# Split weights of the post stage: written to DRAM in the first pass, loaded as parts in the later ones

## The chip, the cores and the metric

The kernel runs on one NeuronCore of a Trainium2 chip. The metric is the device time of one execution in microseconds. The engines are TensorE (PE: matrix products), VectorE (DVE), ScalarE (ACT), GpSimd (POOL) and SyncE (SP), which issues nearly all DMAs. SBUF is the memory on the chip, PSUM holds the accumulators of PE, and DRAM is the memory outside.

## The reference

One layer of a bidirectional encoder, float32, 2048 tokens of 1024 numbers:

```
y = rmsnorm(h, norm_mix_g) @ w_in                  # q, k, v (8 heads of 64), conv input and gate
att  = dilated_sliding_attention(q, k, v)          # three windows: (128,1), (512,4), (2048,16)
conv = conformer_conv(a, g, ...)                   # gated, 31 taps, layernorm, silu
h = h + concat([att, conv]) @ w_out
xq = rmsnorm(h, norm_x_g) @ w_xq;  mn = rmsnorm(mem, norm_mem_g)     # 256 memory rows, 4 heads of 256
h = h + softmax(xq (mn @ w_xk)^T / 16) (mn @ w_xv) @ w_xo
u = rmsnorm(h, norm_mlp_g) @ w_up                  # 1024 -> 4096
h = h + square(relu(u)) @ w_down                   # 4096 -> 1024
return rmsnorm(h, norm_final_g)
```

## The kernel before

Every product is made in float32 quality from float16 parts. A number is held as a high part and a low part (what the high part leaves over), both float16, and `mm3` sums three products: high by high, high by low, low by high. Activations and weights are split alike. For a weight tile of 128 x 1024 float32 the split is two instructions in `wsplit2`: ACT writes the scaled tile as float16 (L362), and DVE takes it from the scaled float32 tile and writes the rest as float16 (L363). The two parts together are as large as the float32 tile, 512 KB.

The kernel works in stages. A first stage normalises x, multiplies by `w_in`, prepares the memory side (from w_xq, w_xk, w_xv, w_xo it builds two matrices once, `ascr` and `bscr`, in DRAM) and scans the weights for scales. Attention for the first 512 tokens follows. Then comes the post stage, in four passes `p` of 512 tokens each, function `post(p)`. A pass multiplies by w_out (8 tiles), by the memory matrices a and b (8 tiles each), by w_up (32 tiles) and by w_down (32 tiles), with norms between them. The weights don't fit into SBUF, so each pass loads every tile anew. `wpost` does that:

```
raw = wp.tile(list(shape), F32, tag="raw", name=f"raw_{name}", bufs=3)
dma(raw, src)
n = turn_w[0]
turn_w[0] += 1
return two(wsplit2(wq if n % 4 > 1 else wp, raw, name, scale, shape=shape))
```

There are three buffers for raw tiles and four for split ones: two in the pool `wp`, two in the pool `wq`, taken in turn. One tile serves 24 matmuls of 128x512. `ahead(m)` prepares the first two tiles of w_out while the first attention still runs.

Beside pass `p` run attention (`att`) and convolution (`conv`) of the next 512 tokens, woven in by rate. Attention fills PE where the main work waits, and uses DVE (scores with mask, `att_probs`, L1042), ACT (exponentials L1043), PE (turning L1049, products L1057 to L1059, scores L1260). Convolution is 30 DVE instructions of `cacc` (L392) for each 128 x 512. Before the MLP the norm's chain runs: column sums (nps, L1449), a reciprocal root on DVE and POOL (`rstd_col`: st_v, nr, st_t, L346 to L353), its broadcast on PE (nrb, L358), ACT's copy ssumx (L1577), and then `rl` on DVE (L1596), which reads the accumulator of a w_up tile with that scale.

The last pass, `last_mlp`, has no attention beside it. It multiplies by w_down with seven products instead of eight (`seven`), in seven pieces of 128 x 2 x 512 for each of its first seven groups; `quarter` loads the four quarters of w_down that the pieces are made of, `sums` adds and subtracts them, and `piece` splits the results. `hidden` makes the w_up products.

The program is written in this order, but a scheduler that models time places each instruction in its engine's queue; each engine then runs its queue strictly in order, SP too. A DMA that has to wait holds up all later DMAs of its queue.

Of the kernel before, what the change touches and what calls it, by code (L numbers as in the profile page):

```python
# [12 lines left out]
F16 = mybir.dt.float16  # L13
# [8 lines left out]
P = 128  # L22
# [12 lines left out]
KC = D // P  # L35
# [13 lines left out]
def hybrid_layer(ctx, tc, A, out):  # L49
# [7 lines left out]
    def dma(o, i, q=None):  # L57
        (q or nc.sync).dma_start(o, i)

    dr = pool("dram", DRAM)  # L60
# [55 lines left out]
    cath = [dr.tile([P, S], F16, name=f"cath{k}") for k in range(KC)]  # L116
    catl = [dr.tile([P, S], F16, name=f"catl{k}") for k in range(KC)]
    gscr = [dr.tile([P, 2, 8, P], F16, name=f"gscr{i}") for i in range(8)]
    vscr = dr.tile([P, 2, 8, 256], F16, name="vscr")
    ascr = dr.tile([XH // 2, P, KC, 2 * NMEM], F32, name="ascr")  # L120
    bscr = dr.tile([KC, P, KC, P], F32, name="bscr")
# [92 lines left out]
    S_UP, S_DN, S_OUT, S_A, S_B = (bcol(i) for i in range(5))  # L214
# [3 lines left out]
    K_OUT, K_A, K_B, K_UP, K_DN = (bcol(24 + i) for i in range(5))  # L218
# [139 lines left out]
            PE.transpose(dst_ps[:, j * P:(j + 1) * P], col[:, j:j + 1].to_broadcast([P, P]), ident)  # L358

    def wsplit2(wp, raw, name, scale, shape=(P, 8, P)):  # L360
        t = wp.tile([P, 2, *shape[1:]], F16, tag="ws", name=f"ws_{name}", bufs=2)
        ACT.activation(t[:, 0], raw, AF.Copy, scale=scale)  # L362
        DVE.scalar_tensor_tensor(t[:, 1], raw, scale, t[:, 0], op0=ALU.mult, op1=ALU.subtract)  # L363
        return t

    def two(t):
        return t[:, 0], t[:, 1]

    def wcols(w, c0, n=P, rows=None):
        v = w.rearrange("(k p) m -> p k m", p=P)  # L370
        return v[:, :, c0:c0 + n] if rows is None else v[:, rows[0]:rows[1], c0:c0 + n]
# [7 lines left out]
    w_in, w_out = A["w_in"][0], A["w_out"][0]  # L379
    w_xq, w_xk, w_xv, w_xo = (A[n][0] for n in ("w_xq", "w_xk", "w_xv", "w_xo"))  # L380
    w_up, w_down = A["w_up"][0], A["w_down"][0]
# [73 lines left out]
    wp = pool("weights")  # L455
# [895 lines left out]

    turn_w = [0]

    def wpost(src, name, scale, shape=(P, 8, P)):

        raw = wp.tile(list(shape), F32, tag="raw", name=f"raw_{name}", bufs=3)
        dma(raw, src)
        n = turn_w[0]
        turn_w[0] += 1
        return two(wsplit2(wq if n % 4 > 1 else wp, raw, name, scale, shape=shape))  # L1360

    wout = {}

    def ahead(m):
        yield
        raw = wp.tile([P, 8, P], F32, tag="raw", name=f"raw_o0{m}", bufs=3)
        dma(raw, wcols(w_out, m * P))
        yield
        yield
        wout[m] = two(wsplit2(wp, raw, f"o0{m}", S_OUT))  # L1370
        turn_w[0] += 1
        yield

# [96 lines left out]
    def resid_linear(load, rhs, korder, resid, hs, ssum, scale, gains, y, name, steps=False, wide=False):  # L1470


        for ms in ((0, 1, 2, 3) if wide else (0, 1, 2), () if wide else (3,), (4,), (5,), (6,), (7,)):
            wt = [load(m) for m in ms]
            pts = {}
            cuts = (0, 4, 6, 7, 8) if wide else (0, 4, 6, 8)
            for ks in [korder[a:b] for a, b in zip(cuts, cuts[1:])] if len(ms) > 1 else (korder,):
                for m, (wh, wl) in zip(ms, wt):
                    if m not in pts:
                        pts[m] = ps("m3" if wide and m == 3 else "mm", f"{name}{m}")  # L1480
                    for k in ks:
                        mm3(pts[m], wh[:, k, :], wl[:, k, :], rhs["h", k], rhs["l", k], k == korder[0], k == korder[-1])
                    if steps and ks[-1] != korder[-1]:
                        yield
                    if ks[-1] == korder[-1]:
                        h = hs[m]
                        g = gains[:, m:m + 1]
                        last["dve"] = DVE.scalar_tensor_tensor(h, pts[m], scale, resid(m), op0=ALU.mult, op1=ALU.add)
                        ACT.activation(y["h", m], h, AF.Copy, scale=g)  # L1489
                        DVE.scalar_tensor_tensor(y["l", m], h, g, y["h", m], op0=ALU.mult, op1=ALU.subtract)  # L1490
                        add_sq(h, ssum, m == 0)
                        yield

    def post(p):
# [6 lines left out]
        def from_x(m):  # L1501
# [3 lines left out]

        y = ytiles("y")
        ssum = ssum_tile(f"o{p}")
        yield from resid_linear(lambda m: wout[m] if p == 0 and m in wout else wpost(wcols(w_out, m * P), f"o{p}{m}", S_OUT),
                                cats[p], [4, 5, 6, 7, 0, 1, 2, 3], from_x, hs, ssum, K_OUT, gxm[:, 0:8], y, f"o{p}_",
                                p == 0, p == 0)  # L1510
        rs = rstd_from(ssum)
# [31 lines left out]
        for hp in range(XH // 2):  # L1543
            pth, ptl = (xquad(q, hp, f"pt{q}{p}{hp}") for q in "hl")
            for e in range(4):
                pr_["h", 4 * hp + e], pr_["l", 4 * hp + e] = pth[:, e], ptl[:, e]
            sps = []
            for kk in range(4):
                ah, al = wpost(ascr[hp, :, 2 * kk:2 * kk + 2, :], f"a{p}{hp}{kk}", S_A, (P, 2, 512))
                for t in range(4):  # L1550
                    if kk == 0:
                        sps.append(ps("xs", "xs"))
                    js = slice(P * t, P * t + P)
                    for k2 in range(2):
                        k = 2 * kk + k2
                        mm3(sps[t], y["h", k][:, js], y["l", k][:, js], ah[:, k2, :], al[:, k2, :], k == 0, k == KC - 1)
                    if len(late) > 2 or (late and kk == 0):
                        turn_probs(*late.pop(0))
                    if kk == 3:
                        late.append((pth, ptl, t, soft(sps[t], t)))  # L1560
                yield
# [1 line left out]

        y = ytiles("m")
        ssum = ssum_tile(f"x{p}")
        xl = resid_linear(lambda m: wpost(bscr[m], f"b{p}{m}", S_B), pr_, list(range(KC)), lambda m: hs[m], hs, ssum, K_B,
                          gxm[:, 8:16], y, f"x{p}_", True)
        for _ in range(3):
            next(xl)
# [14 lines left out]
        for fg in range(FG):  # L1584
            hh = {}
            for q in "hl":
                t = xquad(q, fg % 2, f"hh{q}{p}_{fg}")
                for j in range(4):
                    hh[q, j] = t[:, j]
            for c in range(4):  # L1590
                wh, wl = wpost(wcols(w_up, fg * 512 + c * P), f"u{p}{fg}_{c}", S_UP)
                pt = ps("mm", "up")
                for k in range(KC):
                    mm3(pt, wh[:, k, :], wl[:, k, :], y["h", k], y["l", k], k == 0, k == KC - 1)
                r = tmp("rl")
                last["dve"] = DVE.scalar_tensor_tensor(r, pt, 0.0, rsb, op0=ALU.max, op1=ALU.mult)  # L1596
                ACT.activation(r, r, AF.Square)
                ACT.copy(hh["h", c], r)
                DVE.tensor_tensor(hh["l", c], r, hh["h", c], op=ALU.subtract)
                yield  # L1600
            if fg == FG - 1:
                fsum = ssum_tile(f"f{p}")
                load_cat(p + 1, 0)

            def down(mp2, wh, wl):
                for e in range(2):
                    m = 2 * mp2 + e
                    es = slice(P * e, P * e + P)
                    pt = ps("mm", "dn")
                    for k in range(4):  # L1610
                        mm3(pt, wh[:, k, es], wl[:, k, es], hh["h", k], hh["l", k], k == 0, k == 3)
                    last["dve"] = DVE.scalar_tensor_tensor(hs[m], pt, K_DN, hs[m], op0=ALU.mult, op1=ALU.add)  # L1612
                    if fg == FG - 1:
                        add_sq(hs[m], fsum, m == 0)

            for mp2 in range(4):
                down(mp2, *wpost(wcols(w_down, mp2 * 256, 256, (4 * fg, 4 * fg + 4)), f"d{p}{fg}_{mp2}", S_DN, (P, 4, 256)))
                yield


# [20 lines left out]
    def last_mlp(hs, y, rsb):  # L1641
# [24 lines left out]

        def hidden(fg, c):

            wh, wl = wpost(wcols(w_up, fg * 512 + c * P), f"u{p}{fg}_{c}", S_UP)
            pt = ps("up", "up")  # L1670
            for k in range(KC):
                mm3(pt, wh[:, k, :], wl[:, k, :], y["h", k], y["l", k], k == 0, k == KC - 1)
                if fg == 0 and c < 2 and k % 2:
                    to_rows(4 * c + k // 2)
            r = tmp("rl") if c else cv.tile([P, 512], F32, tag="vr", name="rl", bufs=2)
            last["dve"] = DVE.scalar_tensor_tensor(r, pt, 0.0, rsb, op0=ALU.max, op1=ALU.mult)
            ACT.activation(r, r, AF.Square)
            return r
# [42 lines left out]
            return t  # L1721

        def piece(w, name):
            n = turn_w[0]
            turn_w[0] += 1
            return two(wsplit2(wq if n % 4 > 1 else wp, w, name, S_DN, shape=(P, 2, 512)))

        def sums(b):

# [139 lines left out]
```

## Time and profile before

| | |
|---|---|
| time, median of 3 runs | 2739.62 us (2738.18 to 2741.42) |
| the profiled execution | 2743.33 us, of which the span of its instructions is 2741.6 us |
| busy | PE 97%, DVE 75%, ACT 48%, POOL 13% |
| DMA | 413.81 MB, 151 GB/s over the span |
| first w_out product of the post stage | 715.8 us after the start |
| granted clock of PE, mean | 0.988 |

A row of the profile names the line of the kernel, the engine, the operation, what it writes and reads (`out<-in`), shapes and count, then the busy time in us and the mean of one in ns, and behind the last bar the idle time of the engine just before, with what ended it. Matmuls overlap: one of 128x512 is shown as 380 ns long, but one starts every 215 ns, so a busy PE may still be slow when its clock is. `PEclk` is the share of the full clock that PE was granted. In the list of waits, a row says which engine and instruction waited for which, the sum in us, how often, and the longest.

### The profile page before, as it was taken

Reading aid. Unit: us, or ns where it says so; the run is one execution under the profiler, and the core shown is the slowest. Engines: PE = TensorE matmul, PEld = TensorE weight load, DVE = VectorE, ACT = ScalarE, POOL = GpSimd, SP = SyncE. Lnnn points to the kernel's source line nnn. Section 1 sums busy time; section 2 is a strip of 40 time slices with the busy share of each in tenths; the row PEclk is TensorE's granted clock in tenths of the full one; section 3 lists DMA queues with packets and bytes.
Section 4 is the critical chain, followed back from the end, with each engine's and each line's share of the span. In section 5 each row is a group of like instructions: output and inputs, shape, how many; then the busy total and the mean of one; then the engine's idle time right before and its main releaser. Section 6 shows DMA issues by size and latency. Waiting matters only on the chain.

```text
span 2741.6 us, 41228 instructions
## 1 busy us (share of the span) xinstructions
PE 2661.1 (97%) x15514; PEld 1454.8 (53%) x15514; DVE 2047.5 (75%) x3707; ACT 1315.3 (48%) x2185; POOL 345.5 (13%) x405
## 2 busy tenths in 40 slices
PE   8879999999899999999999999999999999999998
PEld 7734446777555445545554554455455544444443
DVE  5675665577689887667988966589887656679997
ACT  5625655376555434434543444355434434445543
POOL 1033201131200110310010113000110210000000
PEclk9979999999999999999999999999999999999999
DMA  9985888756544444445344445444444445223341
GB/s 269 279 209 175 249 254 279 202 146 197 141 132 120 128 129 127 138 135 169 101 129 136 123 127 139 139 145 124 122 123 144 129 138 176 92 86 99 101 123 62
DMA packets 534088, 413.81 MB, mean 151 GB/s; under 512 B 124957, under 2 KB 470993, under 8 KB 533120
## 3 DMA queue, kind: packets, MB, share of 16 engines
q1 hardware_dynamic: 525920, 396.15, 50.3%
q10 hardware_dynamic: 5744, 9.02, 1.0%
q0 software_dynamic: 2224, 6.01, 0.6%
q8 instruction: 122, 2.00, 0.3%
q14 instruction: 78, 0.64, 0.1%
HBM read 342.52 MB, written 68.57 MB: 150 GB/s over the span
## 4 chain that ended last, share of the span: by engine, by line
PE 65%; DVE 8%; DMA 3%; issue 3%; POOL 2%; ACT 1%; SPq 0%; DVEq 0%; POOLq 0%; ACTq 0%
PE dn L375 7%; PE dn L377 7%; PE dn L376 7%; PE up L375 7%; PE up L376 7%; PE up L377 7%; PE pt L1049 2%; PE xs L375 2%; PE xs L376 2%; PE xs L377 2%; DVE cacc L392 2%; PE s L1260 1%; PE o L375 1%; PE o L377 1%; PE o L376 1%
## 5 line engine op out<-in xcount | busy, mean ns | idle before, releaser
L375 PE MATMUL up<-mh,ws_u 128*128 128x512 f16 x1024 | 389.4, 381 | 0.7 <-ACT mh L1489 0.6
L376 PE MATMUL up<-ml,ws_u 128*128 128x512 f16 x1024 | 389.6, 380 | 0.0
L377 PE MATMUL up<-mh,ws_u 128*128 128x512 f16 x1024 | 388.4, 380 | 0.0
L392 DVE SCALAR_TENSOR_TENSOR cacc<-cu,cw,cacc 128x512 f32<-128x512 f32 x480 | 367.0, 765 | 4.9
L377 PE MATMUL dn<-hhh,ws_d 128*128 128x512 f16 x768 | 290.6, 379 | 0.0
L376 PE MATMUL dn<-hhl,ws_d 128*128 128x512 f16 x768 | 290.5, 379 | 0.0
L375 PE MATMUL dn<-hhh,ws_d 128*128 128x512 f16 x768 | 283.0, 379 | 0.9 <-DVE h L1612 0.9
L362 ACT ACTIVATE ws_u<-raw_u,bd 128x1024 f16<-128x1024 f32 x128 | 146.8, 1147 | 236.5 <-PE dn L377 186.9
L362 ACT ACTIVATE ws_d<-raw_d,bd 128x1024 f16<-128x1024 f32 x100 | 114.8, 1148 | 279.6 <-PE up L377 251.5
L1612 DVE SCALAR_TENSOR_TENSOR h<-dn,bd,h 128x512 f32<-128x512 f32 x192 | 140.6, 746 | 62.9 <-PE dn L377 60.1
L363 DVE SCALAR_TENSOR_TENSOR ws_u<-raw_u,bd,ws_u 128x1024 f16<-128x1024 f32 x128 | 163.9, 1280 | 19.3 <-ACT ws_u L362 17.1
L1042 DVE CUSTOM_DVE_ANT_0 sm<-s,mask,qks 128x256 f32<-128x256 f32 (+1 forms) x384 | 150.9, 434 | 30.5 <-PE s L1260 20.1
L377 PEld LDWEIGHTS <-ws_u 128*128 128x128 f16 x1024 | 100.4, 98 | 120.8 <-issue 1.8
L1596 DVE SCALAR_TENSOR_TENSOR rl<-up,ssumx 128x512 f32<-128x512 f32 x96 | 65.7, 690 | 131.1 <-PE up L377 131.1
L375 PEld LDWEIGHTS <-ws_u 128*128 128x128 f16 x1024 | 100.8, 98 | 114.9 <-issue 1.7
L376 PEld LDWEIGHTS <-ws_u 128*128 128x128 f16 x1024 | 101.0, 99 | 113.4 <-issue 1.4
L363 DVE SCALAR_TENSOR_TENSOR ws_d<-raw_d,bd,ws_d 128x1024 f16<-128x1024 f32 x100 | 133.8, 1338 | 31.2 <-ACT ws_d L362 30.6
L1043 ACT ACTIVATE sm<-sm,o 128x256 f32<-128x256 f32 (+1 forms) x288 | 116.3, 453 | 72.8 <-DVE o L1042 72.1
L1053 DVE TENSOR_TENSOR pl<-pt,ph 128x512 f16<-128x512 f32 x160 | 109.3, 685 | 37.4 <-ACT ph L1052 37.2
L377 PEld LDWEIGHTS <-ws_d 128*128 128x128 f16 x768 | 75.1, 98 | 89.1
L1052 ACT CAST ph<-pt 128x512 f16<-128x512 f32 x160 | 91.1, 571 | 60.0 <-PE pt L1049 59.9
L376 PEld LDWEIGHTS <-ws_d 128*128 128x128 f16 x768 | 75.1, 98 | 80.5 <-issue 2.5
(518 smaller groups left out, 6394.9 us busy)
## 6 DMA issues: line engine op xcount, KB each, us to landing
raw_u<-in_w_up_dram SPq DMA_DIRECT2D x128, 512.0 KB
raw_d<-in_w_down_dram SPq DMA_DIRECT2D x100, 512.0 KB
scan<-in_w_up_dram SPq DMA_DIRECT2D x32, 512.0 KB
scan<-in_w_down_dram SPq DMA_DIRECT2D x32, 512.0 KB
raw_o<-in_w_out_dram SPq DMA_DIRECT2D x32, 512.0 KB
raw_a<-ascr SPq DMA_DIRECT2D x32, 512.0 KB
raw_b<-bscr SPq DMA_DIRECT2D x32, 512.0 KB
b<-in_w_down_dram SPq DMA_DIRECT2D x28, 512.0 KB
```

The source lines that it names most:

```text
L362: ACT.activation(t[:, 0], raw, AF.Copy, scale=scale)
L363: DVE.scalar_tensor_tensor(t[:, 1], raw, scale, t[:, 0], op0=ALU.mult, op1=ALU.subtract)
L375: PE.matmul(o, lh, rh, start=first, stop=False, skip_group_check=more)
L376: PE.matmul(o, lh, rl, start=False, stop=False, skip_group_check=more)
L377: last["pe"] = PE.matmul(o, ll, rh, start=False, stop=end, skip_group_check=more)
L392: DVE.scalar_tensor_tensor(acc, u[:, t:t + 512], cw[:, c, t:t + 1], acc, op0=ALU.mult, op1=ALU.add)
L1042: last["dve"] = DVE.tensor_tensor_reduce(dst, so, mask[:, 256 * m:256 * m + nk], SCORE, 3e38, ALU.add, ALU.min, mn)
L1043: last["act"] = ACT.activation(dst, dst, AF.Exp, bias=mn, scale=-1.0)
L1052: ACT.copy(ph, pt)
L1053: DVE.tensor_tensor(pl, pt, ph, op=ALU.subtract)
L1596: last["dve"] = DVE.scalar_tensor_tensor(r, pt, 0.0, rsb, op0=ALU.max, op1=ALU.mult)
L1612: last["dve"] = DVE.scalar_tensor_tensor(hs[m], pt, K_DN, hs[m], op0=ALU.mult, op1=ALU.add)
```

## The change

The first pass still loads and splits every tile, and then writes the two parts to DRAM: 88 new arrays `wst` of 128 x 2048 float16, one for each tile of w_out, a, b, w_up and w_down. Passes 2 to 4 load the parts of a tile from `wst` straight into a split buffer, with no raw tile and no ACT or DVE work. In these passes the tiles take turns over seven buffers, the four split ones and the three that were raw. Tiles that are still split, in the first pass and the w_down pieces of the last, take turns over four. The counter is one for both. The last pass's w_down comes from the float32 weights as before, since its pieces are sums of quarters.

```
+    wst = [dr.tile([P, 2 * 1024], F16, name=f"wst{i}") for i in range(88)]
...
+    def wtile(name, n, shape):
+        i = turn_w[0] % n
+        turn_w[0] += 1
+        pl, tag, bufs = (wp, "ws", 2) if i < 2 else (wq, "ws", 2) if i < 4 else (wp, "raw", 3)
+        return pl.tile([P, 2, *shape[1:]], F16, tag=tag, name=f"ws_{name}", bufs=bufs)
...
-    def wpost(src, name, scale, shape=(P, 8, P)):
+    def wpost(src, name, scale, shape=(P, 8, P), key=None, p=0):
+        if p and key is not None:
+            t = wtile(name, 7, shape)
+            dma(flat(t), wst[key])
+            return two(t)
         raw = wp.tile(list(shape), F32, tag="raw", name=f"raw_{name}", bufs=3)
         dma(raw, src)
-        n = turn_w[0]
-        turn_w[0] += 1
-        return two(wsplit2(wq if n % 4 > 1 else wp, raw, name, scale, shape=shape))
+        t = split_to(wtile(name, 4, shape), raw, scale)
+        if key is not None:
+            dma(wst[key], flat(t))
+        return two(t)
...
-        wout[m] = two(wsplit2(wp, raw, f"o0{m}", S_OUT))
+        t = wsplit2(wp, raw, f"o0{m}", S_OUT)
+        dma(wst[m], flat(t))
+        wout[m] = two(t)
...
-                wh, wl = wpost(wcols(w_up, fg * 512 + c * P), f"u{p}{fg}_{c}", S_UP)
+                wh, wl = wpost(wcols(w_up, fg * 512 + c * P), f"u{p}{fg}_{c}", S_UP, (P, 8, P), 24 + 4 * fg + c, p)
...
         def piece(w, name):
-            n = turn_w[0]
-            turn_w[0] += 1
-            return two(wsplit2(wq if n % 4 > 1 else wp, w, name, S_DN, shape=(P, 2, 512)))
+            return two(split_to(wtile(name, 4, (P, 2, 512)), w, S_DN))
```

`split_to` is the body of `wsplit2` with the tile handed in, and `flat` names a tile's two parts as one row of 2048 in each partition. The other calls of `wpost` get a key and `p` in the same way as the one shown: w_out the keys 0 to 7, a 8 to 15, b 16 to 23, w_up 24 to 55, w_down 56 to 87.

More of the change, by code (lines that the diff above doesn't have):

```diff
@@ L360, in wsplit2, with split_to @@
     def wsplit2(wp, raw, name, scale, shape=(P, 8, P)):
-        t = wp.tile([P, 2, *shape[1:]], F16, tag="ws", name=f"ws_{name}", bufs=2)
+        return split_to(wp.tile([P, 2, *shape[1:]], F16, tag="ws", name=f"ws_{name}", bufs=2), raw, scale)
+    def split_to(t, raw, scale):
         ACT.activation(t[:, 0], raw, AF.Copy, scale=scale)
@@ L1352, in hybrid_layer, with flat @@
     turn_w = [0]
-    def wpost(src, name, scale, shape=(P, 8, P)):
+    def wtile(name, n, shape):
[3 more added lines that the diff above has]
+        return pl.tile([P, 2, *shape[1:]], F16, tag=tag, name=f"ws_{name}", bufs=bufs)
+    def flat(t):
+        return t.rearrange("p h a b -> p (h a b)")
+    def wpost(src, name, scale, shape=(P, 8, P), key=None, p=0):
[3 more added lines that the diff above has]
+            return two(t)
         raw = wp.tile(list(shape), F32, tag="raw", name=f"raw_{name}", bufs=3)
         dma(raw, src)
-        n = turn_w[0]
-        turn_w[0] += 1
-        return two(wsplit2(wq if n % 4 > 1 else wp, raw, name, scale, shape=shape))
+        t = split_to(wtile(name, 4, shape), raw, scale)
+        if key is not None:
+            dma(wst[key], flat(t))
+        return two(t)
     wout = {}
@@ L1507, in post @@
         ssum = ssum_tile(f"o{p}")
-        yield from resid_linear(lambda m: wout[m] if p == 0 and m in wout else wpost(wcols(w_out, m * P), f"o{p}{m}", S_OUT),
+        yield from resid_linear(lambda m: wout[m] if p == 0 and m in wout else wpost(wcols(w_out, m * P), f"o{p}{m}", S_OUT, (P, 8, P), m, p),
                                 cats[p], [4, 5, 6, 7, 0, 1, 2, 3], from_x, hs, ssum, K_OUT, gxm[:, 0:8], y, f"o{p}_",
@@ L1548, in post @@
             for kk in range(4):
-                ah, al = wpost(ascr[hp, :, 2 * kk:2 * kk + 2, :], f"a{p}{hp}{kk}", S_A, (P, 2, 512))
+                ah, al = wpost(ascr[hp, :, 2 * kk:2 * kk + 2, :], f"a{p}{hp}{kk}", S_A, (P, 2, 512), 8 + 4 * hp + kk, p)
                 for t in range(4):
@@ L1565, in post @@
         ssum = ssum_tile(f"x{p}")
-        xl = resid_linear(lambda m: wpost(bscr[m], f"b{p}{m}", S_B), pr_, list(range(KC)), lambda m: hs[m], hs, ssum, K_B,
+        xl = resid_linear(lambda m: wpost(bscr[m], f"b{p}{m}", S_B, (P, 8, P), 16 + m, p), pr_, list(range(KC)), lambda m: hs[m], hs, ssum, K_B,
                           gxm[:, 8:16], y, f"x{p}_", True)
@@ L1616, in post @@
             for mp2 in range(4):
-                down(mp2, *wpost(wcols(w_down, mp2 * 256, 256, (4 * fg, 4 * fg + 4)), f"d{p}{fg}_{mp2}", S_DN, (P, 4, 256)))
+                down(mp2, *wpost(wcols(w_down, mp2 * 256, 256, (4 * fg, 4 * fg + 4)), f"d{p}{fg}_{mp2}", S_DN, (P, 4, 256), 56 + 4 * fg + mp2, p))
                 yield
@@ L1667, in hidden @@
         def hidden(fg, c):
-            wh, wl = wpost(wcols(w_up, fg * 512 + c * P), f"u{p}{fg}_{c}", S_UP)
+            wh, wl = wpost(wcols(w_up, fg * 512 + c * P), f"u{p}{fg}_{c}", S_UP, (P, 8, P), 24 + 4 * fg + c, p)
             pt = ps("up", "up")
```

## The prediction

> **What bounds the kernel now.** I read the page first, then the busy time by stage, then the waits of TensorE (PE) in each pass, then the chain of work around the longest of them.
>
> ```profile
> span 2741.6 us, 41228 instructions
> PE 2661.1 (97%) x15514; PEld 1454.8 (53%) x15514; DVE 2047.5 (75%) x3707; ACT 1315.3 (48%) x2185; POOL 345.5 (13%) x405
> L362 ACT ACTIVATE ws_u<-raw_u,bd 128x1024 f16<-128x1024 f32 x128 | 146.8, 1147 | 236.5 <-PE dn L377 186.9
> L363 DVE SCALAR_TENSOR_TENSOR ws_u<-raw_u,bd,ws_u 128x1024 f16<-128x1024 f32 x128 | 163.9, 1280 | 19.3 <-ACT ws_u L362 17.1
> L363 DVE SCALAR_TENSOR_TENSOR ws_d<-raw_d,bd,ws_d 128x1024 f16<-128x1024 f32 x100 | 133.8, 1338 | 31.2 <-ACT ws_d L362 30.6
> ```
>
> PE is busy for 97% of the span. The two parts of a split (ACT L362, DVE L363) cost 2.4 to 2.5 us a tile, but on other engines, and each idles before its part: ACT 236.5 us for ws_u, until PE frees a tile. Most of what the change deletes therefore lies beside PE. What it can win is only the time in which PE waits or runs slowly, so I look for that stage by stage.
>
> ```profile
> core 0: us, PE busy (x) PEld busy (x) DVE busy (x) ACT busy (x) POOL busy (x), PEclk, DMA share, GB/s
> 300.00:400.00 100.00, 100.00 (x483) 47.51 (x482) 68.62 (x105) 57.41 (x99) 4.92 (x9) 1.00 0.87 258
> 400.00:500.00 100.00, 98.24 (x718) 70.47 (x717) 60.27 (x126) 48.69 (x91) 14.96 (x34) 1.00 0.83 255
> 760.00:1240.00 480.00, 474.47 (x2673) 241.18 (x2672) 382.62 (x635) 218.15 (x341) 61.35 (x63) 1.00 0.45 128
> 778.00:779.00 1.00, 1.00 (x6) 0.47 (x5) 1.00 (x2) 1.00 (x3) 0.00 (x0) 1.00 0.00 0
> 779.00:782.70 3.70, 3.70 (x19) 1.68 (x18) 3.70 (x7) 1.58 (x3) 0.00 (x0) 1.00 0.47 148
> 782.70:783.60 0.90, 0.90 (x8) 0.54 (x5) 0.90 (x1) 0.00 (x0) 0.00 (x0) 1.00 0.00 0
> 893.00:899.00 6.00, 3.82 (x18) 1.91 (x18) 6.00 (x14) 4.79 (x10) 0.61 (x3) 0.77 0.84 209
> 1240.00:1760.00 520.00, 514.77 (x2890) 262.36 (x2889) 404.30 (x672) 235.19 (x365) 61.64 (x64) 1.00 0.46 132
> 1411.00:1419.00 8.00, 5.55 (x23) 2.62 (x23) 8.00 (x18) 6.62 (x13) 2.24 (x4) 0.79 0.76 194
> 1419.00:1430.00 11.00, 11.00 (x61) 5.21 (x60) 6.23 (x10) 3.10 (x5) 4.83 (x4) 1.00 0.30 73
> 1760.00:2280.00 520.00, 516.24 (x2892) 262.62 (x2891) 403.52 (x661) 233.76 (x360) 62.89 (x64) 1.00 0.45 132
> 1930.00:1938.00 8.00, 5.60 (x24) 2.65 (x24) 8.00 (x18) 6.57 (x13) 2.29 (x4) 0.79 0.72 190
> 2500.00:2700.00 200.00, 200.00 (x929) 90.69 (x927) 187.58 (x259) 97.58 (x126) 0.00 (x0) 1.00 0.35 103
> ```
>
> Of each stretch the row gives the time, PE's busy time, then the other engines, PE's granted clock, the DMA share and GB/s. The four passes begin at about 720, 1240, 1760 and 2280 us. PE idles for 5.53 us in the first (480 - 474.47), 5.23 in the second, 3.76 in the third. The bulk of the last pass has no idle time at all (200.00 of 200.00), though DVE is busy for 94% of it. Almost half of what passes 2 and 3 lose sits in one place each, at 1411 and 1930 us; the first pass has the same place at 893 us. There DVE is busy without a gap (8.00 of 8.00), and the clock of PE falls to 0.79. Who waits for whom in the second pass, and what the chain through 1411 us is made of:
>
> ```profile
> PE catT L1205 <- POOL cat L1197: 1.7, 1, 1.7
> PE s L1260 <- DVE low L1042: 1.3, 2, 1.0
> PE opt L1057 <- ACT ph L1052: 0.7, 1, 0.7
> PE pt L1049 <- ACT ssumx L1577: 0.5, 1, 0.5
> ```
>
> ```profile
> by line: DVE cacc L392 24.7%; DVE ws_d L363 15.9%; DVE sm L1042 13.6%; PE up L375 10.5%; PE up L376 8.6%; PE up L377 8.6%; PE s L1260 6.3%; DVE pl L1053 4.0%; issue 3.5%; DVE o L1280 2.3%; DVE st_t L351 1.0%; DVE low L1042 0.8%; DVE st_t L3
> ...
> 1406.44 1.20 DVE ws_d L363
> ...
> 1411.89 1.20 DVE ws_d L363
> ...
> 1414.94 0.94 PE s L1260 x4
> ```
>
> At this place the norm ahead of the MLP has to reach rl (L1596) before PE may reuse its accumulators, so PE has nothing but attention to fill with, and that too hangs on DVE. DVE works off convolution (cacc), scores (sm) and weight splits in turn; two splits of 1.20 us lie on the chain, 2.4 us of it. The last three waits above (1.3, 0.7, 0.5) are this place: 2.5 us together.
>
> **The change, part by part.**
>
> *Splits removed.* Passes 2 and 3 make 88 tiles each (8 w_out, 8 a, 8 b, 32 w_up, 32 w_down), the last pass 56 without its w_down pieces: 232. At 1.147 us that is 266 us of ACT, and at 1.280 (64 tiles of w_down at 1.338) 301 us of DVE. All but the place above lies under PE's work, so I cost it at nothing; the cover is PE's own queue, and it can't go, since these are deletions. What is late next there: in the order of the changed kernel's instructions the reciprocal root's three small DVE operations follow each other directly, the broadcast (nrb) and rl come some 25 matmuls earlier, and no split stands between. So the wait goes in passes 2 and 3. Its price is idle time plus slow clock: 2.45 + 0.21 x 8 = 4.1 us at 1411, and 2.40 + 1.68 = 4.1 at 1930. **-8.2 us.** Bounds: 0 if other DVE work moves into the hole; -9.9 if POOL's catT wait of 1.7 goes too. I take the rows of the two places. In the first pass the splits stay, and the order around 893 us is nearly the old one: nothing gained.
>
> *Writes added.* 88 writes of 0.52 MB make 46 MB, in some 480 us: 96 GB/s on top of 128, so 224 GB/s and a DMA share of about 0.79. The two rows at 300 to 500 us bracket the cost: at 258 GB/s PE lost nothing, at 255 it lost 1.76 us per 100. The second, over 480 us, is 8.4 us against the 5.5 that the pass loses already, 2.9 more. I take +1.0, nearer to the row with the heavier traffic (bounds 0 and 2.9).
>
> *SP's queue.* A write waits on SP for DVE's half of its tile, and all later DMAs of SP are behind it: weight loads, keys, values, residuals, convolution rows. But the order shows each write right in front of the raw load three tiles later, and that load already waits for the same DVE instruction, to free its buffer. So those behind wait no longer than now: 0. In the first pass a tile has then to stay until its write has landed too; the next split into it comes four tiles later, after 72 or more matmuls of 0.215 us (200 us / 929), 15 us: hidden. In passes 2 and 3 a load has seven tiles in turn, six of PE's work ahead, 31 us.
>
> *Loads in the last pass.* Here w_up takes turns of seven and the w_down pieces turns of four over the same tiles, so turns collide. By the order, three w_up loads can only start when PE has left their tile 13, 18 and 19 matmuls before it needs the new one: 2.8, 3.9 and 4.1 us. How long a load takes that is alone:
>
> ```profile
> 779.01 0.32 SPq L58 DMA_DIRECT2D raw_a<-ascr  x1
> ```
>
> and among others, as the chain of waits of the whole run has it:
>
> ```profile
> 665.58 4.61 DMA raw_o<-in_w_out_dram
> ...
> 846.06 9.87 DMA raw_b<-bscr
> ...
> 1376.05 5.74 DMA raw_u<-in_w_up_dram
> ```
>
> The load alone is issued at 779.01, and by 782.70 the DMA engines are idle again (0.00 in the row behind): 3.7 us. At that price PE waits 0.9 + 0 + 0. At 4.61 it is 1.8 + 0.7 + 0.5 = 3.0, at 5.74 6.4, at 9.87 18.9. DMA is at 0.35 in this stage, so I take the first, **+0.9 us**, bounds 0 and 18.9. The Trainium skill ("DMA: Bandwidth & Descriptors", Anatomy of one DMA) gives about 2.0 us fixed plus the bytes at 436 GB/s (a fit for GpSimd's queue), an estimate of 3.2 us for such a tile; by it this term would be 0.4 and the sum half a microsecond better. The 3.7 us of the row decide.
>
> *Sum:* -8.2 + 1.0 + 0.9 = -6.3 us. The profiled execution took 2743.3 us, its span and 1.7 us around it; that gives 2737.0. The median of the runs shown is 2739.6, 3.7 below it, so I forecast **2733.3 us**. A measurement of this kernel can tell about 0.2% from no change, 5.5 us.
>
> **The rivals.**
>
> *The last pass waits for weights (slower).* In the queue of SP, loads of w_down quarters stand directly in front of the first of the three loads, and the order lets PE mix pieces and hidden units matmul by matmul, with much less in hand than the old order, which had whole units of 24 between them. For it: DVE at 94% there, and the row of 9.87 us for a load among others. Against it: no wait at all in 200 us today, DMA at 0.35, and some 30 splits fewer on DVE. Price at 9.87 us a load: -7.2 + 18.9 = +11.7, 2751.3 us. It decides from about 7.8 us a load on (3 x 7.8 - 10.8 = 12.6, which is 5.4 after the 7.2).
>
> *The wait moves (no change).* In the chain the convolution has more time (24.7%) than the splits (15.9%), and DVE's queue is full at that place; if the scores now wait behind convolution rather than splits, nothing is won: +1.9, 2741.5 us. Against it is the order, where one convolution step stands between root and rl.
>
> *The first pass pays (no change).* One raw_u issue stood 8.45 us on SP while the DMA engines were full:
>
> ```profile
> 847.25 8.45 SPq L58 DMA_DIRECT2D raw_u<-in_w_up_dram  x1
> ```
>
> With 75% more traffic that happens oftener. One such hold that uncovers PE gives -8.2 + 8.45 + 0.9 = +1.2, 2740.8 us. The Trainium skill (same page and section) speaks for it: DMA engines don't wait for semaphores, the issuing sequencer does before it dispatches, so 88 more waiting DMAs all hold SP. The trace agrees in that SP stands; but no PE wait follows that row.
>
> That the change doesn't do what it says is excluded by the order: the ACT halves of 232 tiles are gone, and 88 writes are there.
>
> **How the numbers follow.** Forecast 0.46, last pass 0.24, the wait moves 0.14, first pass pays 0.16. The forecast is the only case of the four beyond 0.2% on the fast side, the second the only one on the slow side: faster 0.46, same 0.30, slower 0.24. Low end: all of -9.9, the first pass's own place gone as well (2.18 idle + 0.23 x 6 = 3.6), nothing paid: -13.5, about 2726. High end: short of the price of the slower rival, at loads of 9.1 us, +9.4: 2749. The forecast's own range is 2728 to 2734.
>
> **What would show it.** Right: no slow clock and no DVE wait of PE near 1411 and 1930 us; passes 2 and 3 each about 4 us shorter, the first about 1 longer; ACT down by 266 us and DVE by 301; DMA share near 0.8 in the first pass. Wrong: PE waiting for a DMA into ws_u in the last pass, or for ws_d of DVE; PE waits in the first pass for key or residual loads; the wait for low (L1042) still there under its new line.

## The result, and the profile after

| | before | after |
|---|---|---|
| time, median of 4 runs each | 2740.52 us (2738.18 to 2741.67) | 2753.91 us (2752.22 to 2755.81) |
| ratio | | 1.0049, 95% interval 1.0036 to 1.0062 |
| the profiled execution, and its span | 2743.33, 2741.6 us | 2752.22, 2750.5 us |

The change costs 13.4 us. Forecast were 2733.3 us and a range of 2726 to 2749, so the sign was wrong and the time lies outside the range. The page after shows that the work did leave ACT and DVE, 232 instructions of each and 245 and 264 us of busy time (in which overlapping instructions count once), and that PE does as much as before:

```profile
span 2750.5 us, 40553 instructions
PE 2659.6 (97%) x15514; PEld 1453.0 (53%) x15514; DVE 1783.6 (65%) x3475; ACT 1069.9 (39%) x1953; POOL 322.0 (12%) x405
```

The busy time by stretch of the span splits the result in two. These rows of the kernel after answer to those of before in the prediction:

```profile
core 0: us, PE busy (x) PEld busy (x) DVE busy (x) ACT busy (x) POOL busy (x), PEclk, DMA share, GB/s
760.00:1240.00 480.00, 458.93 (x2568) 232.16 (x2566) 369.09 (x614) 210.27 (x328) 61.81 (x63) 0.98 0.69 213
1240.00:1760.00 520.00, 519.97 (x2930) 265.98 (x2929) 306.46 (x589) 145.49 (x281) 49.86 (x64) 1.00 0.46 138
1760.00:2280.00 520.00, 519.97 (x2922) 265.06 (x2920) 302.02 (x578) 140.81 (x273) 50.32 (x64) 1.00 0.44 133
```

Passes 2 and 3 no longer wait at all: PE is busy for 519.97 of 520 us at full clock, the two places of the norm wait included, where 5.23 and 3.76 us were idle before. The first pass idles for 21.07 us (480 - 458.93), against 5.53 before.

A pass lasts from the first product of its w_out stage to that of the next. By these starts (715.3, 1268.7, 1779.0, 2287.8 and the end of the span after; 715.8, 1244.4, 1763.5, 2278.8 before) the passes took 553.4, 510.3, 508.8 and 462.7 us, against 528.6, 519.1, 515.3 and 462.8. So the first lost 24.8, the next two gained 15.3, the last changed by nothing. Inside the first pass, here are its four stages (w_out, a, b, MLP), cut where the first product of each starts, first of the kernel before, then of the kernel after:

```profile
715.80:766.90 51.10, 45.44 (x283) 23.64 (x280) 35.21 (x71) 24.14 (x40) 5.61 (x8) 0.97 0.63 169
766.90:822.20 55.30, 54.61 (x332) 29.23 (x331) 49.61 (x99) 27.78 (x56) 1.06 (x1) 1.00 0.34 113
822.20:872.30 50.10, 49.51 (x303) 26.48 (x300) 46.87 (x89) 28.43 (x51) 0.59 (x1) 1.00 0.50 132
872.30:1244.40 372.10, 367.85 (x2034) 184.45 (x2033) 283.75 (x448) 159.46 (x234) 59.70 (x61) 1.00 0.46 129
```

```profile
715.30:768.70 53.40, 46.67 (x283) 24.30 (x280) 33.44 (x69) 22.68 (x38) 5.62 (x8) 0.94 0.74 202
768.70:840.90 72.20, 59.86 (x338) 30.54 (x337) 53.99 (x105) 30.36 (x56) 2.63 (x2) 0.91 0.53 182
840.90:891.80 50.90, 49.57 (x293) 26.00 (x293) 42.64 (x82) 27.04 (x50) 0.00 (x0) 1.00 0.60 184
891.80:1268.70 376.90, 369.49 (x2035) 184.98 (x2033) 284.71 (x450) 157.80 (x232) 59.18 (x61) 0.99 0.71 216
```

The a stage (the scores of the memory attention, 8 tiles) takes 72.20 us and not 55.30, with almost the same matmuls (338 and 332). Idle time is 12.34 us against 0.69, and the clock 0.91 against 1.00. That is 16.9 of the 24.8 us; the MLP has 4.8, w_out 2.3, b 0.8. The stage's mean DMA share, 0.53, looks harmless. In slices of 20 us it doesn't; before, then after:

```profile
760.00:780.00 20.00, 19.31 (x103) 9.19 (x102) 18.21 (x24) 11.10 (x16) 0.00 (x0) 1.00 0.47 153
800.00:820.00 20.00, 20.00 (x118) 10.94 (x117) 17.17 (x33) 9.56 (x18) 0.00 (x0) 1.00 0.28 90
```

```profile
760.00:780.00 20.00, 18.18 (x100) 8.87 (x98) 11.77 (x16) 8.60 (x11) 0.00 (x0) 1.00 0.97 344
780.00:800.00 20.00, 19.62 (x108) 9.59 (x106) 17.95 (x28) 8.08 (x11) 0.00 (x0) 1.00 0.26 91
800.00:820.00 20.00, 10.91 (x48) 5.06 (x49) 16.30 (x47) 8.04 (x22) 2.04 (x1) 0.66 0.69 213
803.00:813.00 10.00, 3.26 (x21) 1.84 (x22) 8.75 (x27) 5.07 (x12) 0.00 (x0) 0.54 0.95 347
```

From 760 to 780 us the DMA engines are full (0.97, 344 GB/s), and DVE, busy for 18.21 of those 20 us before, now does 11.77. PE pays 20 us and more later: from 800 to 820 us it makes 48 matmuls in place of 118. By then the engines are nearly full once more (0.95 from 803 to 813 us, the last row). The chain of waits of the kernel after joins the two:

```profile
758.89 9.18 DMA raw_a<-ascr
768.17 1.16 ACT ws_a L365
769.36 1.30 DVE ws_a L366
770.67 0.32 SPq L58
...
771.51 6.62 DMA res<-xscr
778.16 0.76 DVE h L1508
...
784.84 4.83 DMA res<-xscr
789.70 0.75 DVE h L1508
...
796.89 1.29 DVE ws_a L366
798.19 0.32 SPq L58
798.56 6.06 DMA raw_a<-ascr
804.73 1.16 ACT ws_a L365
...
807.63 4.04 DMA raw_b<-bscr
811.84 0.75 ACT xp L1546 x3
812.63 0.59 PE xs L378
813.22 0.43 PE xs L379
```

From 758.89 to 812.63 us no matmul is on it. A raw load takes 9.18 us to land; ACT and DVE split it; the split lets SP go on, which sends the write and behind it the next load, a residual; DVE, strictly in order, stands for that residual (6.62, then 4.83 us), and what it does late (convolution, then the next split at 796.89) makes the next raw load late. It is one round of load, DVE, SP, load. The step from the load of raw_b to xp is the profile's inference, and a weak one, since xp reads nothing of that tile; the list of ACT's waits puts xp's own wait down to DVE's xmx (1.9 us, longest 1.5). How PE comes into it is in the waits of ACT and DVE for DMAs (715 to 850 us) and of PE (a stage), all of the kernel after:

```profile
ACT ws_a L365 <- DMA raw_a<-ascr: 11.9, 4, 7.8
...
DVE h L1508 <- DMA res<-xscr: 6.2, 4, 2.4
...
PE opt L1060 <- ACT ph L1055: 5.6, 1, 5.6
PE xs L378 <- ACT xp L1546: 2.2, 1, 2.2
PE o L378 <- DVE h L1508: 1.8, 1, 1.8
```

and ACT's wait for the same tile in the kernel before:

```profile
ACT ws_a L362 <- DMA raw_a<-ascr: 1.9, 1, 1.9
```

From 1.9 us in one place it has grown to 11.9 in four, and behind a waiting split stand, in ACT's queue, the attention's `ph` and the softmax's `xp`, for which PE waits. PE's longest wait here is the 5.6 us for `ph`; from 803 to 813 us its granted clock is 0.54, and the matmuls that follow start every 0.43 us (813.22 on) and not every 0.22, until the clock is back. The Trainium skill ("TensorE: Matmul & The Clock Gate", Part 1) says that after about 3.4 us of idle time PE runs at half clock, and the 128x512 matmul then starts every 426.7 ns; the 5.6 us and the 0.43 us here agree.

### The profile page after: what moved, and what is told of

Its sections match the earlier page's. It is cut to its first block, busy times and chain, and to the rows that moved or that the text cites. A ratio compares the mean times of both kernels' runs of the same rounds, so it can differ in the third digit from the quotient of the medians.

```text
span 2750.5 us, 40553 instructions
## 1 busy us (share of the span) xinstructions
PE 2659.6 (97%) x15514; PEld 1453.0 (53%) x15514; DVE 1783.6 (65%) x3475; ACT 1069.9 (39%) x1953; POOL 322.0 (12%) x405
## 4 chain that ended last, share of the span: by engine, by line
PE 83%; DMA 7%; DVE 5%; ACT 2%; issue 1%; POOL 1%; SPq 1%; DVEq 0%; POOLq 0%; ACTq 0%
PE up L378 8%; PE up L379 8%; PE up L380 8%; PE dn L378 7%; PE dn L380 7%; PE dn L379 7%; PE lin L378 3%; PE lin L379 3%; PE lin L380 3%; PE pt L1052 2%; PE x L379 2%; PE x L380 2%; PE x L378 2%; PE xs L378 2%; PE xs L379 2%; PE xs L380 2%
## 5 line engine op out<-in xcount | busy, mean ns | idle before, releaser
L1617 ACT ACTIVATE rl<-rl 128x512 f32<-128x512 f32 x96 | 60.2, 627 | 236.2 <-DVE rl L1616 236.2
L380 PEld LDWEIGHTS <-ws_d 128*128 128x128 f16 x768 | 75.1, 98 | 89.1
L379 PEld LDWEIGHTS <-ws_d 128*128 128x128 f16 x768 | 75.1, 98 | 81.3 <-issue 1.5
L378 PEld LDWEIGHTS <-ws_d 128*128 128x128 f16 x768 | 74.6, 98 | 79.4
L351 POOL TENSOR_TENSOR nr<-st_v,mhalf 128x4 f32<-128x4 f32 (+1 forms) x15 | 14.4, 960 | 826.3 <-DVE st_v L347 825.9
L1052 PE MATMUL pt<-ident,sm 128*128 128x128 f32 x640 | 99.3, 275 | 7.4 <-ACT sm L1046 5.1
```

Source lines behind the costliest of these rows:

```text
L378: PE.matmul(o, lh, rh, start=first, stop=False, skip_group_check=more)
L379: PE.matmul(o, lh, rl, start=False, stop=False, skip_group_check=more)
L380: last["pe"] = PE.matmul(o, ll, rh, start=False, stop=end, skip_group_check=more)
L1052: last["pe"] = PE.transpose(pt[:, j, :], sm[:, j, :], ident)
```

## The experiments

Times of stages come from one profiled execution, which lies up to 6 us from the median of its kernel. The scheduler plans each kernel anew, so the queues of two kernels also differ outside the edit. Each ratio is to runs of the kernel before on the same chip. Stages of the first pass and passes 1 to 3, in us:

| kernel | time | ratio to before (95%) | w_out, a, b, MLP | passes 1, 2, 3 |
|---|---|---|---|---|
| before | 2740.52 | | 51.1, 55.3, 50.1, 372.1 | 528.6, 519.1, 515.3 |
| after | 2753.91 | 1.0049 (1.0036 to 1.0062) | 53.4, 72.2, 50.9, 376.9 | 553.4, 510.3, 508.8 |
| writes alone | 2764.97 | 1.0091 (1.0074 to 1.0108) | 52.6, 72.1, 51.0, 377.2 | 552.9, 516.7, 513.3 |
| loads alone | 2726.36 | 0.9957 (0.9942 to 0.9971) | 53.0, 54.7, 50.1, 372.4 | 530.2, 510.4, 508.7 |
| writes from POOL | 2745.35 | 1.0024 (1.0015 to 1.0034) | 54.3, 69.9, 51.7, 373.0 | 548.9, 510.4, 508.7 |
| small writes | 2730.31 | 0.9964 (0.9951 to 0.9977) | 50.5, 55.2, 50.2, 373.7 | 529.6, 510.4, 508.7 |
| MLP only | 2730.98 | 0.9976 (0.9966 to 0.9986) | 53.1, 55.3, 50.2, 374.2 | 532.8, 511.7, 510.5 |
| MLP only, from POOL | 2732.63 | 0.9980 (0.9971 to 0.9989) | 52.7, 56.0, 50.1, 370.9 | 529.7, 511.3, 510.4 |
| side written in pass 2 | 2731.87 | 0.9979 (0.9969 to 0.9988) | 52.2, 54.8, 50.2, 377.1 | 534.3, 514.4, 508.8 |
| w_out and MLP | 2739.14 | 0.9999 (0.9989 to 1.0008) | 50.9, 55.5, 49.7, 373.7 | 529.8, 511.3, 510.0 |
| a and MLP | 2736.95 | 0.9990 (0.9979 to 1.0001) | 50.8, 58.8, 50.2, 375.4 | 535.2, 512.6, 511.1 |
| b and MLP | 2734.31 | 0.9982 (0.9972 to 0.9991) | 52.7, 55.0, 50.1, 377.3 | 535.1, 510.9, 509.9 |
| fourth raw buffer | 2743.95 | 1.0018 (1.0009 to 1.0028) | 52.2, 68.6, 50.8, 375.7 | 547.3, 510.3, 508.8 |
| before, fourth raw buffer | 2736.35 | 0.9992 (0.9982 to 1.0001) | 52.6, 54.4, 50.2, 369.1 | 526.3, 515.6, 515.6 |

**The two halves of the change.** *Writes alone*: the later passes split as before.

```
-        if p and key is not None:
+        if False:
...
-        if key is not None:
+        if key is not None and not p:
             dma(wst[key], flat(t))
```

> The first pass splits and writes its 88 tiles as in the changed kernel; the later passes split every tile as before. Between the two kernels the first pass grew by 24.8 us, the second and third shrank by 8.8 and 6.5. If the writes alone cost the first pass that time, this kernel takes 2740.5 + 25 = 2765 us. If the first pass is longer because the later passes' lighter order moved work into it, it takes about 2742.

*Loads alone*: nothing is written; the later passes load as many bytes from eight arrays that an earlier stage left in DRAM.

```
-            dma(flat(t), wst[key])
+            dma(flat(t), flat(gscr[key % 8]))
...
-            dma(wst[key], flat(t))
+            pass
...
-        dma(wst[m], flat(t))
```

> No writes; the later passes load as many bytes, as split parts, from eight float16 tiles that the first stage left in DRAM, so their weights are the wrong ones. If gain and cost are separate: 2740.5 - 15 = 2725 us, first pass as before (528.6 us), second and third at 510 and 509. If part of the loss lies in the loads (turns of seven and four over the same tiles), it stays above 2732.

The writes alone cost 25.3 us (2764.97 against 2739.69 of before on the same chip), the loads alone win 13.3. Together +12.0, where the change as a whole cost 13.4: the halves add up, within intervals of some 4 us each. With the loads alone PE is busy for 519.97 of 520 us from 1240 us on, as in the kernel after, and the first pass is that of before (530.2 and 528.6 us). The whole loss is made by the writes, in the first pass.

**SP's queue, or the bytes.** *Writes from POOL*: the same 88 writes, issued from POOL's queue, so that none holds SP.

```
-            dma(wst[key], flat(t))
+            dma(wst[key], flat(t), POOL)
...
-        dma(wst[m], flat(t))
+        dma(wst[m], flat(t), POOL)
```

> The changed kernel with its 88 writes issued by POOL in place of SP; the bytes, and the tiles that are held until they land, are the same. Theory A (SP stands behind each write until DVE has split the tile, and residual loads, raw loads and keys queue behind it): 2730 to 2735 us, the memory-attention stage of the first pass back at about 55 us from 72. Theory B (the DMA engines are full with 46 MB more in that stage, 0.97 at 760 to 780 us, and loads land late): 2750 to 2758, that stage still about 72 us.

*Small writes*: all writes stay on SP, with their waits, but move 32 bytes per partition and not 4096; the later passes load as in the loads alone.

```
-            dma(wst[key], flat(t))
+            dma(wst[key][:, 0:16], flat(t)[:, 0:16])
...
-        dma(wst[m], flat(t))
+        dma(wst[m][:, 0:16], flat(t)[:, 0:16])
...
-            dma(flat(t), wst[key])
+            dma(flat(t), flat(gscr[key % 8]))
```

> The writes stay on SP with the same waits, but each carries 32 bytes of a partition in place of 4096; the later passes load from the first stage's float16 tiles as in the kernel with loads alone, so the weights are the wrong ones there. Theory A (SP held by the waits): near the changed kernel, 2748 to 2755 us. Theory B (bytes): near the kernel with loads alone, 2725 to 2730.

From POOL the a stage still takes 69.9 us; with small writes it takes 55.2, as before. The slices of 760 to 780 us say why, first with the writes from POOL, then with the small ones:

```profile
760.00:780.00 20.00, 17.64 (x98) 8.66 (x97) 13.81 (x21) 9.46 (x14) 2.65 (x5) 1.00 0.99 361
```

```profile
760.00:780.00 20.00, 19.36 (x107) 9.68 (x106) 18.10 (x26) 8.68 (x12) 0.00 (x0) 1.00 0.54 160
```

The bytes fill the DMA engines, from whichever queue they are issued. The Trainium skill ("DMA: Bandwidth & Descriptors", Rules for kernel authors) says that DMAs of SP, ACT and GpSimd all run on the same 16 engines, so that another issuing engine brings no bandwidth: that agrees, at 0.99 of the engines. That SP is held is not the cause in this stage, and small writes with all their waits on SP cost 1.9 us by the ratios (0.9964 against 0.9957 of the loads alone), which the intervals can't tell from nothing.

Yet neither theory had foreseen 2745.35 us: it lies between their times, nearer to the bytes by the stage that loses most. By the ratios (1.0024 against 1.0049, intervals that just don't meet) issuing the full writes from POOL saves about 7 us. The two profiles show 4.5 us of that in the first pass, 3.9 of them in the MLP (373.0 against 376.9 us). One wait of PE goes with it there: for POOL's `cat` (L1200) PE waits once, 2.7 to 3.2 us, in each of the eight kernels of the table that write the MLP's tiles from SP, 0.9 to 1.3 us in the four that don't move these bytes, and not at all in the two that write from POOL. What `cat` is late for was not followed, so the cause of this part stays open.

**Which tiles, and which pass.** *MLP only*: the 24 tiles of w_out, a and b are split in every pass, only w_up and w_down (64 tiles) are written and loaded.

```
-        if p and key is not None:
+        if p and key is not None and key > 23:
...
-        if key is not None:
+        if key is not None and key > 23:
             dma(wst[key], flat(t))
...
-        dma(wst[m], flat(t))
```

> Only the 64 tiles of w_up and w_down are written and loaded; the 24 of w_out, a and b are split in every pass as before. If the first pass loses its time because the writes of w_out and a meet residual loads, raw loads, keys and convolution rows in the same 20 us, its memory-attention stage goes from 72 back to 55 us, the MLP stage stays 5 us longer, passes 2 and 3 keep their gain but for a microsecond each: 2740 - 13 + 1.5 + 5 = 2733 us. If any writes cost in proportion to their bytes, 64/88 of the 25 us stay: 2746.

This version beats both kernels: 2730.98 us, 6.8 less than before on the same chip (ratio 0.9976). The a stage is back at 55.3 us. It writes 64 of the 88 tiles, and yet 24.8 us of loss in the first pass become 4.2: the cost is not in proportion to the bytes. *MLP only, from POOL* is the same with `dma(wst[key], flat(t), POOL)`:

> As the kernel with the MLP's tiles alone, its 64 writes issued by POOL. With all 88 written from POOL the first pass's MLP stage was 373.0 us against 376.9 from SP and 372.1 before. If that 4 us is SP being held, this kernel comes to 2740 - 13 + 1.5 + 1 = 2729 us; if not, it stays at 2733.

The MLP of the first pass takes 370.9 us in the profile, 3.3 less than from SP, but the median, 2732.63 us, is no better than 2730.98. In the profile the last pass is 3.3 us longer than in the MLP only (466.4 against 463.1), 3.0 of them behind DVE's last instruction at the very end; why is not known. A gain from issuing these 64 writes from POOL isn't shown.

*Side written in pass 2*: the 24 tiles are split and written in the second pass and loaded in passes 3 and 4.

```
-        if p and key is not None:
+        if key is not None and p > (key < 24):
...
-        if key is not None:
+        if key is not None and p == (key < 24):
             dma(wst[key], flat(t))
...
-        dma(wst[m], flat(t))
```

> As the kernel with the MLP's tiles alone, but w_out, a and b are split and written in the second pass and loaded in the third and fourth. If the tightness belongs to the first pass (which starts with no weights ahead and DVE full), the second pass's memory-attention stage stays near 50 us and the time is 2732 to 2734 us. If it belongs to that stage in any pass, it grows by some 15 us there: 2748.

It is as fast as the MLP only. The same writes of w_out and a meet the same loads of a and of the residual there, and PE loses nothing in these two stages (46.5 and 49.3 us, as in the MLP only); the pass as a whole takes 514.4 us against 511.7. Here are the 20 us of that kernel in pass 2 that lie ahead of its a stage, which starts at 1295.4 us:

```profile
1270.00:1290.00 20.00, 20.00 (x110) 10.76 (x109) 14.13 (x23) 10.93 (x16) 0.00 (x0) 1.00 0.99 369
```

The engines are as full there as in the first pass of the kernel after (0.99 and 0.97) and move more (369 and 344 GB/s), and PE is busy for all of the 20 us. So full engines alone don't make the loss. What differs is how long ahead the loads are issued: the first load of an a tile 25.6 us before the first product of the a stage here (1269.87 and 1295.42 us), 12.8 us in the first pass of the kernel after (755.91 and 768.72). Just ahead of the loads in the first pass SP's queue is held by the first attention's output, in both kernels (waits of the DMA queue, 715 to 765 us, before and after):

```profile
SPq L58 <- DVE cat L1197: 13.9, 1, 13.9
```

```profile
SPq L58 <- DVE cat L1200: 14.6, 1, 14.6
```

At the start of pass 2 (1249 to 1300 us) SP's longest single wait is 5.4 us. Behind the hold in the first pass the keys, the residuals and the raw tiles are all issued within a few microseconds. That it is this late start which makes full engines cost PE time is argued from these rows, not tried by itself.

**Whose writes.** The next three are the MLP only, with the writes and loads of one more group of eight: of w_out (`key < 8 or key > 23`, with the writes of `ahead`), of a (`8 <= key < 16 or key > 23`), of b (`key > 15`).

> Of the 24 small writes of the first pass (w_out, a, b) only the 8 of w_out are made, with all those of w_up and w_down; the later passes load the same ones and split a and b as before. The full set costs 24.8 us of the first pass, 17 of it in the memory-attention stage, and with none of the 24 the stage takes 49 to 55 us as before. Theory 'a burst': the stage loses time only when the writes of w_out and those of a fall together with the loads of a and of the residual at 757 to 780 us; one group alone leaves the DMA engines below full there (0.52 to 0.54 without writes, 0.97 with both, so about 0.7), the stage takes 55 to 60 us, and the kernel 2729 to 2735 us. Rival 'each byte counts': a third of the loss for a third of the tiles, stage 60 us or over and kernel 2736 us or more.

> Of the 24 small writes only the 8 of the a tiles are made, with all of w_up and w_down. Theory 'a burst': DMA share of 760 to 780 us below 0.9, the memory-attention stage 55 to 60 us, kernel 2729 to 2735 us. Rival 'each byte counts': stage about 60 us, kernel 2736 to 2740. A second rival: the stage's own writes are all that matters (they sit in SP's queue and on the DMA engines between its own loads), then the stage takes 68 us or more as with all 24, and the kernel 2743 us or more.

> Of the 24 small writes only the 8 of the b tiles are made, with all of w_up and w_down. They are issued from about 800 us on, behind the burst. Theory 'a burst': the memory-attention stage takes 50 to 55 us, as without any of them, and the kernel 2726 to 2732 us, the 8 loads in place of splits in each later pass gaining a little. Rival 'each byte counts': 2736 us or more.

The slices of 760 to 780 us with w_out's writes, then with a's; between them w_out's from 750 to 770 us:

```profile
760.00:780.00 20.00, 20.00 (x108) 9.68 (x107) 16.46 (x22) 10.40 (x14) 0.00 (x0) 1.00 0.73 254
```

```profile
750.00:770.00 20.00, 19.88 (x103) 9.29 (x103) 16.63 (x21) 12.68 (x18) 0.00 (x0) 1.00 0.95 314
```

```profile
760.00:780.00 20.00, 17.40 (x89) 8.03 (x88) 15.61 (x21) 8.51 (x12) 0.00 (x0) 0.95 0.69 225
```

By the ratios times 2740 us, the MLP only is 6.6 us under before; with w_out it is 0.3 under, with a 2.7, with b 4.9. So the groups cost 6.3, 3.9 and 1.7 us, together 11.9, where all three cost 13.4 + 6.6 = 20.0.

The burst theory is half right. The a stage takes 55.5, 58.8 and 55.0 us with one group and 72.2 with all three, as it said: in that stage the loss, but for 3.5 us with a's group, appears only when the groups come together. But its condition, that one group leaves the engines below full, fails for w_out: they are at 0.95 from 750 to 770 us, around the start of the a stage (765.4), and the loads of a are issued as late as in the kernel after (12.8 us ahead), and the stage loses nothing. And the times of all three (2739.14, 2736.95, 2734.31) are above what the theory allowed (2735, 2735, 2732), the first two within the range of its rival. With intervals of some 2.7 us either way these shares are rough: the cost of b's group can't be told from nothing, and the 8 us by which the whole exceeds the sum have an interval about as wide as themselves. The profile of w_out's run, of an execution of 2733.2 us, shows only some 3 us of its loss, in the last pass (465.8 us), where PE waits 2.4 us for `h` in the a stage.

**The buffers.** *Fourth raw buffer*: the kernel after, with a buffer more for the raw tiles of the first pass.

```
+        if key is not None and key % 4 == 3:
+            raw = wq.tile(list(shape), F32, tag="raw4", name=f"raw_{name}", bufs=1)
+        else:
             raw = wp.tile(list(shape), F32, tag="raw", name=f"raw_{name}", bufs=3)
```

> The changed kernel with all its writes and loads, but every fourth raw tile of the stored weights in the first pass has a buffer of its own (one of 4 KB a partition in a pool that is open anyway), so that a raw load waits for the split four tiles earlier and not three. Theory 'a round of load, split and next load': the writes make each load of a tile land later, the split behind it waits, and with it the load that needs its buffer; with a fourth tile in hand the round has a third more time, the memory-attention stage falls from 72 us to 62 or below, and the kernel from 2754 us to 2744 or below. Rival 'the engines are full': what is lost at 757 to 780 us is lost by the bytes, whatever the buffers; the stage stays at 68 us or over and the kernel at 2748 us or more. The list scheduler moves a few matmuls of neighbouring stages with the buffer, so 2 us either way mean nothing.

Its control is the kernel before with the same buffer, taken at every fourth turn:

> The control: the kernel before with the same fourth raw buffer in its first pass, every fourth tile by its turn. No wait for a raw load of more than 1.9 us stands in that stage before the change, so both theories expect no gain: within 4 us of before. If it gains 8 us or more, the fourth buffer helps by something other than the writes, and the run with the writes says little.

The time came out as the theory of the round said (2743.95 us), the stage as its rival said (68.6 us). The wait that the buffer was meant for did go; ACT's wait for a raw tile in this kernel, 715 to 850 us, and the chain in the stage:

```profile
ACT ws_a L365 <- DMA raw_a<-ascr: 1.3, 1, 1.3
```

```profile
760.12 7.75 DMA res<-xscr
767.90 0.76 DVE h L1511
...
777.46 6.55 DMA res<-xscr
784.03 0.75 DVE h L1511
```

11.9 us of waiting became 1.3, yet the residual loads, in engines busy for 0.82 of 760 to 780 us, still land after 7.75 and 6.55 us, and DVE still stands for them. So the round through the raw buffers is one way in which the late loads reach PE, and not the only one. Of the ratio's fall from 1.0049 to 1.0018 (8.5 us), 2.2 us (1 - 0.9992) may be the buffer's own, which the control can't tell from nothing.

## Why the prediction was wrong

*Splits removed: -8.2 us, bounds 0 and -9.9.* The mechanism was right and its size too small: 13.3 us by the loads alone (7.9 to 15.9 by the interval of the ratio), and 15.3 by passes 2 and 3 of the kernel before. Against the other two kernels that split in these passes (writes alone; before with the fourth buffer) the two passes gain 10.9 and 12.1, so part of the 15.3 is the plan of one kernel. The norm wait and the slow clock are gone at both places, as said. But I priced only these two places. With the splits off ACT and DVE the small waits went as well: 5.2 and 3.8 us of idle time fell to 0.03 each, and with 1.7 us of slow clock twice that is 12.3 of the 15.3. The bound of -9.9 had left the small ones standing.

*Writes added: +1.0 us, bounds 0 and 2.9.* This is the step that failed: 24.8 us by the two profiles, 25.3 by the writes alone. The traffic was, if anything, estimated too high (224 GB/s and a share of 0.79; measured 213 and 0.69). What was wrong was to price it by two rows of 100 us from another stage, and by the mean of a pass. At 300 to 400 us PE stood a share of 0.87 without loss. In the a stage of the first pass, loads of a and of the residual hang on DVE's queue, and DVE's queue on them; there the writes of w_out, a and b together cost 17 us. The row of 0.47 at 760 to 780 us before, with the writes' own 512 KB a tile to add (twice 0.47 is 0.94), would have warned of full engines. It would not have given the price: engines as full cost nothing in pass 2 where the side is written there. Why it is 17 us in the first pass is shown as far as the round above goes, and argued for the late start of the loads; what else it takes stays open.

*SP's queue: 0.* Right for the stage that loses most: small writes with the same waits cost it nothing. For the whole kernel it is open: the 88 writes cost about 7 us less from POOL by the ratios, up to 4 us of it in the MLP, but with the MLP's 64 writes the median gained nothing. "In the first pass a tile has then to stay until its write has landed too": the 15 us taken there did not always hide that. ACT waits three times for a write to land in the MLP of the first pass, 10.3 us together:

```profile
ACT ws_d L365 <- DMA wst<-ws_d: 6.0, 2, 3.2
ACT ws_u L365 <- DMA wst<-ws_u: 4.3, 1, 4.3
```

No such wait stands in the a stage, none at all in the two kernels that write from POOL, and no wait of PE is put down to one.

*Loads in the last pass: +0.9 us, bounds 0 and 18.9.* Right: 462.7 us after, 462.8 before. All that PE waits for a load there:

```profile
PE up L378 <- DMA ws_u<-wst: 0.7, 2, 0.5
```

*The rivals.* The slower one named 2751.3 us, near the truth, by a mechanism that isn't there: the last pass waits 0.7 us, not 18.9. "The wait moves" is excluded by 519.97 of 520 us. "The first pass pays" had the right pass, with a wrong mechanism (SP held, one raw_u load, 8.45 us) and a third of the price; over those 8.45 us of the kernel before, the DMA share was 0.67, so the engines were full for a part of them only. What the text named as signs of an error, PE waits in the first pass for residuals, came, one engine removed: PE waits for ACT and DVE, which wait for the loads.

## What to carry to other kernels

Price added traffic in the slice where it falls, some 20 us wide, not by the mean of a stage: the a stage's 0.53 hid 0.97. Then look how long ahead of their use the loads of that slice are issued, for the share alone doesn't price it: 0.99 cost nothing in one pass, 0.97 was followed by a loss of 17 us in another. Where loads, an engine that works in order and the next loads form a round, full DMA engines can delay every station of it, and PE pays later, at another instruction and under another name. When a spill pays back over several passes, write it where there is room: the 64 tiles of the MLP, or the other 24 a pass later, made a loss of 13.4 us into a gain of about 6.

## What the runs showed of the hardware that was not expected

A 512 KB load that took 3.7 us alone took 9.18 us among reads and writes at a DMA share of 0.97; but one of 9.87 us stands in the kernel before too, at a share of 0.49 (842 to 858 us), so a late load needs no 20 us of full engines. Over 20 us the engines moved 344 to 369 GB/s when full (0.97 to 0.99), with 128-partition loads and stores mixed, whether the stores were issued by SP (344, 369) or by POOL (361).
